# Values by pairs of heads in column groups, norms broadcast by transposes, later weight stores and another order of parts in a two-layer hybrid decoder trunk

## The chip, the cores and the metric

The kernel runs on 1 core of one Trainium2 chip. Its time is the device time of one execution in microseconds (us); lower is better. The engines are TensorE (PE in the profile; PEld is its weight load), VectorE (DVE), ScalarE (ACT), GpSimd (POOL) and SyncE (SP), which issues the DMAs.

## The reference

Two layers, each with a half-step feed-forward, a mixer of four head groups beside each other, and a second half-step feed-forward. x is 512 tokens by 1024, everything in float32.

```python
def hybrid_layer(x, ...):
    x = x + 0.5 * swiglu(rmsnorm(x, ffn1_norm), ffn1_gate, ffn1_up, ffn1_down)   # 1024 -> 2816 -> 1024
    z = rmsnorm(x, mix_norm) @ w_in
    ...
    y_a = dsa_mixer(...)    # per query the best 128 keys by an indexer, 4 heads of 64, T5 bias
    y_b = gla_mixer(...)    # gated linear attention in chunks
    y_c = conv_mixer(...)   # gated causal depthwise convolution, 31 taps
    y_d = mla_mixer(...)    # latent attention, 4 heads, values 64 wide
    x = x + concat([y_a, y_b, y_c, y_d]) @ w_out
    x = x + 0.5 * swiglu(rmsnorm(x, ffn2_norm), ffn2_gate, ffn2_up, ffn2_down)
    return x

# in both attentions, for each block of 128 queries:
    p = jax.nn.softmax(logits, axis=-1)
    return jnp.einsum('bhts,bshd->bthd', p.astype(v.dtype), v)
```

rmsnorm(x) is x * rsqrt(mean(x*x) + 1e-6) * g.

## The kernel before, in words

**Layout.** Activations lie transposed: X[k] holds 128 features by 512 tokens, k from 0 to 7. A large product is done as three passes in a rounded float32 form (fp32r): each operand is split into a high and a low part (hi, lo; `split`, L553), and hi*hi, hi*lo and lo*hi are added up in PSUM (`mm3`, L548). One such pass is one instruction of 128x512. The names of the profile: gu (gate and up) and dn (down) are the feed-forward's products, whl the split weights, xh and xl the split activations, iq, cq, ckv, cg, ca, bq, bk and g the projections of the mixers, wo the output projection, uq and ukv the second projections of attention D's queries and keys. Small products, such as those with the values, are plain float32; one of them shows as two instructions in the profile.

**Stages.** `ffn` (L688) runs 22 blocks of 128 hidden features in four parts; `mixers` (L727) projects, runs the four groups and projects back; the norm of the next stage is summed as X is written. `Norm.finish` (L620) makes the factor per token, r4, and `bcast` (L585) spreads it over the partitions as a row (bc, in the profile rbc): VectorE multiplies the identity by each column (rbcd), and PE multiplies a matrix of ones by that, 512 columns in plain float32 (rbcp). `c_out` (L1185) does the same for the convolution's norm (rcbp).

**Weights of the mixers.** They are loaded early, split once, and stored in device memory in split form (`keep`, L522: kraw, khl, kept), so that `fetch` (L538) can load them split when the mixers need them. In layer 0 the first feed-forward does three of these per hidden block (`ahead=3`, L1268), from its first block on; kraw shares its four buffers with the weights of the feed-forward (raw).

**Attention.** `d_attention(i)` (L967) and `a_attention(i)` (L1207) handle the 128 queries of block i, with 128*(i+1) keys. Per head: logits on PE (dlg; alg and blg, two heads side by side in row groups of the array), row maximum on VectorE (mx), exponential and row sum on ScalarE (dpr, apr; sm), then `attend` (L799): transposes on PE (dpT, apT), a copy to SBUF (pts), the product with the values with pts held in the array and 64 value columns streamed (dpo, apo), and a copy scaled by the reciprocal of the row sum (rs) into y (dy, ay). After four heads `y_out` (L757) transposes y (yT) and splits it into Y for wo. `best(i)` (L843) finds the 128 best keys in 16 rounds of two VectorE instructions (MAX, MATCH_REPLACE) over 128*(i+1) columns; attention A's block i needs it. Logits dlg and alg share two PSUM banks (tag s1), dpT and dpo share two others (s2), projections have four (mm).

**What sets the order.** Nothing is issued as it is written. The program records all its instructions (`Plan.record`, L179); `Plan.schedule` (L289) lays them on the engines by a table of costs and of delays between engines (`EDGE`, L102), with its own idea of the clock (`STAY`, `WAKE`, L107) and of buffers, in rounds; `Plan.run` (L420) issues the order of the round that the plan reckons shortest. The list `ORDER` (L50) gives the parts of the mixers in the order in which they are recorded, and by that the order in which they take turns at shared buffers. On each engine, instructions then run in that order.

Of the kernel before, what the change touches and what calls it, by code (L numbers as in the profile page):

```python
# [19 lines left out]
OP = mybir.AluOpType  # L20
# [20 lines left out]
RAW = 4  # L41
ROUNDS = 5
TMP = {"lg": 4, "t1": 2, "t2": 3, "ct": 1, "dd": 2, "qe": 2, "pts": 2, "yt": 3, "hp": 2, "z3": 4,  "cg": 1, "rbc": 2}
BANKS = {"mm": 4, "s1": 2, "s2": 2}
# [4 lines left out]

ORDER = ("index0 conv0 gates d_tables index1 index_keys best2 d_latent_kv best3 b_decays d_latent best1 "  # L50
         "d_queries d_keys d_room b_heads d_attention0 d_attention2 conv1 d_attention3 d_attention1 "
         "b_states a_heads b_zero b_scores3 values b_scores4 b_scores0 b_halves b_chain b_scores1 "
         "b_scores2 c_out a_bias b_out2 b_out1 a_attention3 b_out3 b_out0 b_gates a_attention0 "
         "a_attention1 b_norm a_attention2").split()

# [36 lines left out]
class _Op:  # L92
    __slots__ = ("args", "forms", "key", "cost", "lat", "tiles", "after", "succ", "n", "work", "port")


class Plan:
# [4 lines left out]

    EDGE = {"VV": 127, "VS": 128, "VP": 256, "VG": 155, "SV": 142, "SS": 220, "SP": 271, "SG": 170,  # L102
            "PV": 196, "PS": 197, "PP": 0, "PG": 200, "GV": 74, "GS": 110, "GP": 203, "GG": 102,
            "DD": 0, "VD": 150, "SD": 150, "PD": 150, "GD": 150, "DV": 170, "DS": 170, "DP": 170, "DG": 170}
    HOLD, MARGIN, KEEP = 300.0, 2000.0, "V"
    TAX = {"V": 400.0, "G": 0.0, "S": 0.0}
    WINDOW, STAY, WAKE = 4096 / 1.2, 0.37, 0.77  # L107

# [70 lines left out]
    def record(self, forms, others=(), whole=None):  # L179

        op = _Op()
        op.n = len(self.ops)
        op.forms = {f[0]: whole or (self.cost(f[0], f[1], *f[3:]),) + f[2:] for f in forms}
        op.port = {f[0] for f in forms if self.shares(f[0], f[1], f[3], f[4])}
        key, method, _, args, kw = forms[0]
        op.key, op.cost = key, op.forms[key][0]
        op.lat, op.work = 0.0, 1.0
        if method == "matmul":
# [100 lines left out]
    def schedule(self, rank):  # L289
# [14 lines left out]
        port, other = {"V": 0.0, "G": 0.0}, {"V": "G", "G": "V"}  # L304
        wire = 0.0
        left = [len(op.after) for op in ops]
# [5 lines left out]
        def choose(e):  # L312
            now, found, first = free[e], [], 1e18
            for op in ready[e]:
# [3 lines left out]
                if e in op.port and t < port[e]:  # L318
                    t = port[e]
                if t > first + self.HOLD:  # L320
                    continue
# [38 lines left out]
        while len(order) < len(ops):  # L360
# [13 lines left out]
            start[op.n] = at  # L374
            cost = op.forms[e][0]
            if e == "P":
                while at >= mark:
# [42 lines left out]
    def run(self):  # L420
# [7 lines left out]
        best = None  # L428
        for _ in range(ROUNDS):
            rank[:self.head] = [n - 1e9 for n in range(self.head)]  # L430
            time, order, start, stop, taken = self.schedule(rank)
            if best is None or time < best[0]:
# [11 lines left out]
def hybrid_trunk(ctx, tc, x_in, cst, masks, onehot, relb, pcol, prow, gu17, w_uq, w_ukv,  # L444
# [140 lines left out]
    def bcast(col, name):  # L585

        dg = tmp("pts", name + "d")
        for i in range(NT):
            V.tensor_scalar(dg[:, i * 128:(i + 1) * 128], ident, col[:, i:i + 1], None, op0=OP.mult)
        ps = bank(name + "p")  # L590
        PE.matmul(ps, ones, dg, start=True, stop=True)
        r = tmp("rbc", name)
        copy(r, ps)
        return r
# [54 lines left out]
    def build_consts():  # L649
        SP.dma_start(ck, cst)  # L650
        for l in range(1, depth):
            SP.dma_start(PC[l], pcol[l])
        V.tensor_copy(identb, ident)
        V.tensor_copy(causb, CM[:, 384:512])

    def build_masks():
        mk = tmp("hp", "mk", 640)
# [29 lines left out]

    def ffn(norm, gu, dn, after, between=lambda: None, lead=(), ahead=0):  # L688

# [9 lines left out]
        for part, n in enumerate(PARTS):  # L699
            H = []  # L700
            for m in range(m0, m0 + n):
# [10 lines left out]
                H.append((hh, hl))  # L712
                keep(ahead)
            for d in range(KD):
# [12 lines left out]
    def mixers(l, norm, after):  # L727
# [70 lines left out]

        def attend(i, h, probs, sm, values, y, name):  # L799
            W = 128 * (i + 1)  # L800
            pt = bank(name + "pT")
            for j in range(i + 1):
                PE.transpose(pt[:, j * 128:(j + 1) * 128], probs[:, j * 128:(j + 1) * 128], ident)
            rs = small("rs", 1, 4)
            V.reciprocal(rs, sm)
            pts = tmp("pts", "pts")
            copy(pts[:, :W], pt[:, :W])
            po = bank(name + "po")
            for j in range(i + 1):
                PE.matmul(po[:, :64], pts[:, j * 128:(j + 1) * 128], values(j, h), start=(j == 0), stop=(j == i))  # L810
            copy(y[:, h * 64:(h + 1) * 64], po[:, :64], rs)

# [154 lines left out]
        def d_attention(i):  # L967

            W = 128 * (i + 1)
            y = tmp("yt", "dy", 256)  # L970
            for h in range(4):
# [6 lines left out]
                S.activation(e[:, :W], p[:, :W], AF.Exp, bias=mx, accum_out=sm)  # L978
                attend(i, h, e, sm, lambda j, h: st.KV[j][:, h, 64:128], y, "d")
            y_out(y, 6, i)  # L980

# [225 lines left out]
        def a_attention(i):  # L1207

            W = 128 * (i + 1)
            y = tmp("yt", "ay", 256)  # L1210
            for h in range(4):
# [13 lines left out]
                S.activation(e[:, :W], e[:, :W], AF.Exp, bias=mx, scale=-1.0, accum_out=sm)  # L1225
                attend(i, h, e, sm, lambda j, h: st.VAB[j][:, h * 64:(h + 1) * 64], y, "a")
            y_out(y, 0, i)

# [162 lines left out]
```

## Time and profile before

| what | value |
|---|---|
| time, median of 3 runs | 2016.08 us (2015.13 to 2018.04) |
| the profiled execution: time, span | 2027.9 us, 2026.1 us |
| mean granted TensorE clock | 0.986 |
| busy: PE, DVE, ACT | 1993.3, 1271.3, 804.0 us |
| moved by DMA | 309.47 MB, mean 153 GB/s |
| ACT_TABLE_LOAD | 10 instructions, 1283 ns each |

How to read it: the span runs from the first to the last instruction of the profiled execution. Busy shares are means over stages with different limits: the four feed-forward stages and the two mixers (about 380 to 660 us and 1383 to 1660 us) have to be looked at apart. The granted clock is the share of full speed that TensorE ran at; at 0.5 a product takes twice as long and PE counts as busy all the while. A wait is put down to what came last.

### The profile page before, as it was taken

To read this page: it belongs to the slowest core of one execution; us is meant where nothing else is said; L and a number is where in the kernel's file an instruction comes from. 1 tells how busy PE (TensorE), PEld (TensorE's weight loads), DVE (VectorE), ACT (ScalarE), POOL (GpSimd) and SP (SyncE) were. 2 spreads that over 40 slices of the span, in tenths; PEclk is the share of its full clock that TensorE was granted. 3 is DMA by queue.
4 is the path that set the end of the run, shared out by engine and by line. 5 is a ranking of instruction groups with operands and counts; after the bars stand their busy time and mean duration, and the time that the engine had idled before them with its cause. 6 is when DMAs were issued, how large, how long until landed. Compare 5 with 4: busy or idle time off the path is not lost.

```text
span 2026.1 us, 26063 instructions
## 1 busy us (share of the span) xinstructions
PE 1993.3 (98%) x9428; PEld 1634.4 (81%) x9430; DVE 1271.3 (63%) x2709; ACT 804.0 (40%) x1566; POOL 7.4 (0%) x20
## 2 busy tenths in 40 slices
PE   8999999999999999999999999999999999999999
PEld 6888888877887888888888888888768778888887
DVE  7665555689895645454675546557889855454544
ACT  5343333365454423333443434333645443222322
POOL 0000000000000000000000000000000000000000
PEclk9999999989899999999999999999989999999999
DMA  8776766552332435353464737446424322323232
GB/s 309 256 259 215 233 202 213 172 165 94 109 131 94 151 118 181 117 172 116 144 218 154 227 112 257 130 146 179 153 81 125 115 94 86 108 89 113 81 107 83
DMA packets 110852, 309.47 MB, mean 153 GB/s; under 512 B 13122, under 2 KB 24676, under 8 KB 110724
## 3 DMA queue, kind: packets, MB, share of 16 engines
q1 hardware_dynamic: 110724, 307.81, 47.3%
q8 instruction: 74, 1.21, 0.2%
q14 instruction: 54, 0.44, 0.1%
HBM read 238.95 MB, written 65.67 MB: 150 GB/s over the span
## 4 chain that ended last, share of the span: by engine, by line
PE 91%; DVE 4%; ACT 2%; DMA 2%; issue 1%; SPq 0%; DVEq 0%; ACTq 0%
PE gu L440 44%; PE dn L440 24%; PE g L440 5%; PE wo L440 5%; PE cq L440 1%; PE iq L440 1%; PE cg L440 1%; PE dlg L440 1%; PE apo L440 1%; PE dpo L440 1%; PE alg L122 1%; PE ca L440 1%; DVE sc L440 1%; PE uq L440 1%; DVE c L440 1%; DMA kraw<-wo 1%
## 5 line engine op out<-in xcount | busy, mean ns | idle before, releaser
L440 PE MATMUL gu<-xh,whl 128*128 128x512 f32 x2816 | 828.6, 391 | 8.0 <-ACT whl L440 6.5
L440 PEld LDWEIGHTS gu<-xh,whl 128*128 128x128 f32 x2816 | 528.8, 188 | 120.7 <-ACT whl L440 6.5
L440 ACT ACTIVATE whl<-raw 128x512 fp32r<-128x512 f32 (+1 forms) x519 | 307.1, 594 | 670.0 <-PE gu L440 363.8
L440 PE MATMUL gu<-xl,whl 128*128 128x512 f32 x1408 | 499.0, 391 | 0.0
L440 DVE TENSOR_TENSOR whl<-raw,whl 128x512 fp32r<-128x512 f32 x576 | 369.4, 646 | 157.2 <-ACT whl L440 151.8
L440 PE MATMUL dn<-hh,whl 128*128 128x512 f32 x1408 | 426.8, 389 | 0.0
L440 PEld LDWEIGHTS gu<-xl,whl 128*128 128x128 f32 x1408 | 264.6, 188 | 55.6 <-issue 0.5
L440 PEld LDWEIGHTS dn<-hh,whl 128*128 128x128 f32 x1408 | 264.1, 188 | 55.7 <-ACT hh L440 0.5
L440 PE MATMUL dn<-hl,whl 128*128 128x512 f32 x704 | 258.4, 389 | 0.0
L440 DVE SCALAR_TENSOR_TENSOR x<-dn,x 128x512 f32<-128x512 f32 x128 | 87.8, 690 | 144.6 <-PE dn L440 144.5
L440 PEld LDWEIGHTS dn<-hl,whl 128*128 128x128 f32 x704 | 132.1, 188 | 28.0 <-issue 0.8
L440 DVE TENSOR_TENSOR fg<-gu,rbc 128x512 f32<-128x512 f32 x88 | 60.6, 689 | 120.1 <-PE gu L440 116.3
L440 DVE TENSOR_TENSOR fu<-gu,rbc 128x512 f32<-128x512 f32 x88 | 60.6, 689 | 97.4 <-PE gu L440 97.3
L440 DVE TENSOR_TENSOR khl<-kraw,khl 128x512 fp32r<-128x512 f32 (+1 forms) x124 | 81.7, 666 | 58.8 <-ACT khl L440 58.3
L440 ACT ACTIVATE khl<-kraw 128x512 fp32r<-128x512 f32 (+1 forms) x123 | 74.9, 613 | 104.0 <-DMA kept<-khl 30.9
L440 PE MATMUL g<-whl,xh 128*128 128x512 f32 (+1 forms) x384 | 101.1, 378 | 0.0
L440 ACT ACTIVATE hh<-fu 128x512 fp32r<-128x512 f32 x86 | 54.5, 634 | 95.3 <-DVE fu L440 95.0
L440 PE MATMUL wo<-yh,whl 128*128 128x512 f32 x256 | 83.1, 415 | 1.4 <-ACT yh L440 1.4
L440 DVE TENSOR_TENSOR hl<-fu,hh 128x512 fp32r<-128x512 f32 x88 | 60.7, 690 | 26.1 <-ACT hh L440 25.4
L440 PEld LDWEIGHTS g<-whl,xh 128*128 128x128 f32 x384 | 68.1, 191 | 9.2 <-ACT bd L440 0.2
L440 ACT ACTIVATE fg<-fg 128x512 f32<-128x512 f32 x88 | 55.3, 629 | 33.3 <-DVE fg L440 30.7
L440 DVE TENSOR_TENSOR fu<-fu,fg 128x512 f32<-128x512 f32 x88 | 60.5, 687 | 2.1 <-ACT fg L440 0.7
(325 smaller groups left out, 1989.6 us busy)
## 6 DMA issues: line engine op xcount, KB each, us to landing
raw<-gu SPq DMA_DIRECT2D x176, 512.0 KB, 4.3
kept<-khl SPq DMA_DIRECT2D x108, 512.0 KB, 4.3
whl<-kept SPq DMA_DIRECT2D x108, 512.0 KB, 3.7
raw<-dn SPq DMA_DIRECT2D x96, 384.0 KB, 3.2
kraw<-wt SPq DMA_DIRECT2D x44, 256.0 KB, 3.7
kraw<-wg SPq DMA_DIRECT2D x32, 256.0 KB, 5.2
kraw<-wo SPq DMA_DIRECT2D x32, 256.0 KB, 4.2
raw<-dn SPq DMA_DIRECT2D x32, 256.0 KB, 2.8
```

Source lines behind the costliest of these rows:

```text
L122: f[2](*f[3], **f[4])
L440: call(*args, **kw)
```

## The change

**Values.** `attend` is split in two. `weigh` takes the reciprocal, scales the probabilities by it, transposes them and copies them to pts. After every second head the new `attend` holds the two heads' values (128 keys by 64) in the two column halves of the array and streams each head's pts (128 queries), so that the outputs of two heads come out transposed, one in partitions 0 to 63 and one in 64 to 127, and are split straight into Y. The copies dy and ay, the buffer yt and the transposes yT of both attentions go (the one of group B stays). pts gets a third buffer.

**Broadcast.** `bcast` makes the row by four PE transposes of a column read 128 times over; the product with ones and its four multiplications go.

**Start.** The constants are loaded in two pieces, the 128 columns of the identity first, and `keep` begins with the third hidden block (`since=2`).

**Plan.** Other delays between engines, another pair of clock thresholds, and a price for a change of table on ScalarE: an activation whose table is not the loaded one is put off by 1280 in the plan's reckoning. Four rounds instead of five, and the fourth one's order is taken (`PICK = 3`) whatever the plan reckons of it. `ORDER` is another permutation: best3 comes ahead of best2 and best1, the kv part of attention D after its query part, a_heads after b_scores3, and attention A's blocks in the order 2, 0, 1, 3 instead of 3, 0, 1, 2.

```diff
-ROUNDS = 5
-TMP = {... "pts": 2, "yt": 3, ...}
+ROUNDS, PICK = 4, 3
+TMP = {... "pts": 3, ...}
...
-    EDGE = {"VV": 127, "VS": 128, "VP": 256, "VG": 155, "SV": 142, "SS": 220, "SP": 271, "SG": 170,
+    EDGE = {"VV": 127, "VS": 128, "VP": 160, "VG": 155, "SV": 142, "SS": 220, "SP": 170, "SG": 170,
...
-    WINDOW, STAY, WAKE = 4096 / 1.2, 0.37, 0.77
+    WINDOW, STAY, WAKE = 4096 / 1.2, 0.40, 0.76
+    TABLES, SWITCH = {AF.Exp: 1, AF.Tanh: 1, AF.Silu: 2, AF.Ln: 3}, 1280.0
...
+                if e == "S" and op.table and op.table != table and t < now + self.SWITCH:
+                    t = now + self.SWITCH
...
     def bcast(col, name):
-        dg = tmp("pts", name + "d")
+        ps = bank(name + "p")
         for i in range(NT):
-            V.tensor_scalar(dg[:, i * 128:(i + 1) * 128], ident, col[:, i:i + 1], None, op0=OP.mult)
-        ps = bank(name + "p")
-        PE.matmul(ps, ones, dg, start=True, stop=True)
+            PE.transpose(ps[:, i * 128:(i + 1) * 128], col[:, i:i + 1].to_broadcast([128, 128]), ident)
...
     def build_consts():
-        SP.dma_start(ck, cst)
+        SP.dma_start(ident, cst[:, C_ID:C_ID + 128])
+
+    def build_masks():
+        SP.dma_start(ck[:, 128:], cst[:, 128:])
...
-                keep(ahead)
+                if m >= since:
+                    keep(ahead)
...
-        def attend(i, h, probs, sm, values, y, name):
+        def weigh(i, probs, sm, name):
             W = 128 * (i + 1)
+            rs = small("rs", 1, 4)
+            V.reciprocal(rs, sm)
+            copy(probs[:, :W], probs[:, :W], rs)
             pt = bank(name + "pT")
             for j in range(i + 1):
                 PE.transpose(pt[:, j * 128:(j + 1) * 128], probs[:, j * 128:(j + 1) * 128], ident)
-            rs = small("rs", 1, 4)
-            V.reciprocal(rs, sm)
             pts = tmp("pts", "pts")
             copy(pts[:, :W], pt[:, :W])
+            return pts
+
+        def attend(i, pts, values, y, name):
             po = bank(name + "po")
-            for j in range(i + 1):
-                PE.matmul(po[:, :64], pts[:, j * 128:(j + 1) * 128], values(j, h), start=(j == 0), stop=(j == i))
-            copy(y[:, h * 64:(h + 1) * 64], po[:, :64], rs)
+            plan.together(200 + 2 * 150 * (i + 1),
+                          *[PE.form("matmul", po[64 * n:64 * n + 64, :128], values(j, n), pts[n][:, j * 128:(j + 1) * 128],
+                                    start=(j == 0), stop=(j == i)) for j in range(i + 1) for n in range(2)])
+            t = slice(i * 128, (i + 1) * 128)
+            split(po[:, :128], y[0][:, t], y[1][:, t])
...
-            y_out(y, 6, i)
+                pts.append(weigh(i, e, sm, "d"))
+                if h % 2:
+                    attend(i, pts[h - 1:], lambda j, n: st.KV[j][:, h - 1 + n, 64:128], Y[6 + h // 2], "d")
...
-            ffn(norm, gu1[l], dn1[l], nm.add, build_masks, lead, ahead=3)
+            ffn(norm, gu1[l], dn1[l], nm.add, build_masks, lead, ahead=3, since=2)
```

How the order moves is shown at three places of layer 0.

The first is on ScalarE, at the gates of group B (la: a logarithm of a sigmoid, by way of Exp and Ln; bcum: its running sum; kd: exponentials of it) and the split of the weights for attention D's queries (shi is the high part that PE's uq holds). Before:

```order
L440 ACTIVATE la_886<-la_886 128x512
L440 ACT_TABLE_LOAD
L440 ACTIVATE la_886<-la_886 128x512
L440 ACTIVATE lsq<-cq 128x512 x2
L440 ACTIVATE rl<-isc 128x256 x2
L440 ACTIVATE bcum<-bcum 128x512
L440 ACTIVATE rl<-isc 128x256
L440 ACTIVATE cqh<-cq,pc_71 128x512
L440 ACT_TABLE_LOAD
L440 ACTIVATE kd<-bcum 128x128 x3
L440 ACTIVATE shi<-raw 128x384
```

The same place now:

```order
L446 ACTIVATE la_890<-la_890 128x512
L446 ACT_TABLE_LOAD
L446 ACTIVATE la_890<-la_890 128x512
L446 ACTIVATE lsq<-ckv 128x512
L446 ACTIVATE bcum<-bcum 128x512
L446 ACTIVATE ckvh<-ckv,pc_71 128x512
L446 ACTIVATE shi<-raw 128x384 x2
L446 ACTIVATE dq<-uq,cqu 128x384 x4
```

The third table load and the three kd moved behind both shi; they now come after the copies dkv of attention D's keys. The indexer's rl of the 256-wide block moved away too.

The second place is on PE, at attention D's block of 512 keys (dlg the logits, the product of causb and identb adds the mask, dpT the transposes, dpo the values). Before:

```order
L440 MATMUL dlg<-dkT_1001,dqT_966 128x512
L440 LDWEIGHTS identb
L440 MATMUL dlg<-causb,identb 128x128
L440 MATMUL dpT<-ck,dpr 128x128 x4
L440 MATMUL dlg<-dkT_1002,dqT_967 128x512
L440 LDWEIGHTS identb
L440 MATMUL dlg<-causb,identb 128x128
L440 MATMUL dpo<-dkv,pts 128x64 x3
L440 MATMUL dpT<-ck,dpr 128x128 x4
L440 MATMUL dpo<-dkv,pts 128x64
L440 MATMUL dlg<-dkT_1003,dqT_968 128x512
```

Now, at the end of the same block's logits and the start of the next block's:

```order
L446 MATMUL dlg<-dkT_1009,dqT_932 128x512
L446 MATMUL dpT<-ck,dpr 128x128 x4
L446 LDWEIGHTS identb
L446 MATMUL dlg<-causb,identb 128x128
L446 MATMUL g_1185<-whl,xl_707 128x512
L446 MATMUL g_1187<-whl,xh_700 128x512
L446 MATMUL g_1188<-whl,xh_700 128x512
L446 MATMUL g_1186<-whl,xh_706 128x512
L446 MATMUL dlg<-dkT_1006,dqT_929 128x384
L446 MATMUL dpT<-ck,dpr 128x128 x4
```

The projection products g (attention A's queries and keys) moved in among attention D's: 31 of them stand ahead of the first dlg and 88 between the first dlg and the last dpo. Before, the first g came after three of the four blocks.

The third place is on VectorE, where attention A begins (ISA apr,mx is the fused bias and row maximum of one head). Before, it stood among the parts of group B:

```order
L440 SCALAR_TENSOR_TENSOR yl_1312<-cth,yh_1311 128x512
L440 ISA apr,mx<-alg,z_1317 128x512
L440 ISA mx 128x1
L440 ISA apr,mx<-blg,z_1318 128x512
L440 ISA mx 128x1
L440 TENSOR_REDUCE bss<-bsq 128x4
L440 RECIPROCAL rs<-sm 128x1
```

Now:

```order
L446 MATCH_REPLACE sc_953<-c_976,sc_953 128x256
L446 ISA apr,mx<-alg,z_1304 128x384
L446 ISA mx 128x1
L446 ISA apr,mx<-blg,z_1305 128x384
L446 ISA mx 128x1
L446 COPY bon<-bo 128x256
L446 RECIPROCAL rs<-sm 128x1
L446 MAX c_977<-sc_953 128x8
L446 RECIPROCAL rs<-sm 128x1
L446 MATCH_REPLACE sc_953<-c_977,sc_953 128x256
```

The 256-wide rounds of best1, which before ran beside attention D, moved to the start of attention A, whose first block is now the one of 384 keys.

More of the change, by code (lines that the diff above doesn't have):

```diff
@@ L41 @@
 RAW = 4
-ROUNDS = 5
-TMP = {"lg": 4, "t1": 2, "t2": 3, "ct": 1, "dd": 2, "qe": 2, "pts": 2, "yt": 3, "hp": 2, "z3": 4,  "cg": 1, "rbc": 2}
+ROUNDS, PICK = 4, 3
+TMP = {"lg": 4, "t1": 2, "t2": 3, "ct": 1, "dd": 2, "qe": 2, "pts": 3, "hp": 2, "z3": 4,  "cg": 1, "rbc": 2}
 BANKS = {"mm": 4, "s1": 2, "s2": 2}
@@ L48 @@
 GROUPS, EARLY = ((6, 7), (4, 5), (2, 3), (0, 1)), (0, 1)
[L50 to L54, printed above, removed]
+ORDER = ("index0 conv0 gates index1 index_keys best3 best2 d_latent d_tables b_decays d_latent_kv "
+         "d_queries b_heads best1 d_keys d_room d_attention1 conv1 d_attention3 d_attention2 d_attention0 "
+         "b_zero b_scores3 a_heads b_states values b_scores4 b_halves b_scores0 b_chain b_scores1 c_out "
+         "b_scores2 b_gates b_out2 b_out0 b_out3 a_bias a_attention2 a_attention0 b_out1 a_attention1 "
+         "b_norm a_attention3").split()
 AQ, AK, AV = 0, 256, 512
@@ L92 @@
 class _Op:
-    __slots__ = ("args", "forms", "key", "cost", "lat", "tiles", "after", "succ", "n", "work", "port")
+    __slots__ = ("args", "forms", "key", "cost", "lat", "tiles", "after", "succ", "n", "work", "port", "table")
 class Plan:
-    EDGE = {"VV": 127, "VS": 128, "VP": 256, "VG": 155, "SV": 142, "SS": 220, "SP": 271, "SG": 170,
+    EDGE = {"VV": 127, "VS": 128, "VP": 160, "VG": 155, "SV": 142, "SS": 220, "SP": 170, "SG": 170,
             "PV": 196, "PS": 197, "PP": 0, "PG": 200, "GV": 74, "GS": 110, "GP": 203, "GG": 102,
@@ L187, in record @@
         op.lat, op.work = 0.0, 1.0
+        op.table = self.TABLES.get(args[2]) if method == "activation" else None
         if method == "matmul":
@@ L304, in schedule @@
         port, other = {"V": 0.0, "G": 0.0}, {"V": "G", "G": "V"}
-        wire = 0.0
+        wire, table = 0.0, None
         left = [len(op.after) for op in ops]
@@ L375, in schedule @@
             cost = op.forms[e][0]
+            if e == "S" and op.table:
+                table = op.table
             if e == "P":
@@ L428, in run @@
         best = None
-        for _ in range(ROUNDS):
+        for turn in range(ROUNDS):
             rank[:self.head] = [n - 1e9 for n in range(self.head)]
             time, order, start, stop, taken = self.schedule(rank)
-            if best is None or time < best[0]:
+            if turn == PICK if PICK is not None else best is None or time < best[0]:
                 best = (time, order, taken)
@@ L654, in build_consts @@
         V.tensor_copy(causb, CM[:, 384:512])
-    def build_masks():
         mk = tmp("hp", "mk", 640)
@@ L685, in rel_bias_tiles, with ffn @@
         return Z
-    def ffn(norm, gu, dn, after, between=lambda: None, lead=(), ahead=0):
+    def ffn(norm, gu, dn, after, between=lambda: None, lead=(), ahead=0, since=0):
         lead, m0 = list(lead), 0
@@ L969, in d_attention @@
             W = 128 * (i + 1)
-            y = tmp("yt", "dy", 256)
+            pts = []
             for h in range(4):
@@ L978, in d_attention @@
                 S.activation(e[:, :W], p[:, :W], AF.Exp, bias=mx, accum_out=sm)
-                attend(i, h, e, sm, lambda j, h: st.KV[j][:, h, 64:128], y, "d")
-            y_out(y, 6, i)
+                pts.append(weigh(i, e, sm, "d"))
+                if h % 2:
+                    attend(i, pts[h - 1:], lambda j, n: st.KV[j][:, h - 1 + n, 64:128], Y[6 + h // 2], "d")
         def b_heads():
@@ L1209, in a_attention @@
             W = 128 * (i + 1)
-            y = tmp("yt", "ay", 256)
+            pts = []
             for h in range(4):
@@ L1225, in a_attention @@
                 S.activation(e[:, :W], e[:, :W], AF.Exp, bias=mx, scale=-1.0, accum_out=sm)
-                attend(i, h, e, sm, lambda j, h: st.VAB[j][:, h * 64:(h + 1) * 64], y, "a")
-            y_out(y, 0, i)
+                pts.append(weigh(i, e, sm, "a"))
+                if h % 2:
+                    attend(i, pts[h - 1:], lambda j, n: st.VAB[j][:, (h - 1 + n) * 64:(h + n) * 64], Y[h // 2], "a")
         parts = dict(gates=gates, index_keys=index_keys, d_latent=d_latent, d_latent_kv=d_latent_kv, d_tables=d_tables, d_queries=d_queries,
```

## The prediction

> **What bounds the kernel now.** I read the page first: the share of each engine and the chain that ended last.
>
> ```profile
> span 2026.1 us, 26063 instructions
> ...
> PE 1993.3 (98%) x9428; PEld 1634.4 (81%) x9430; DVE 1271.3 (63%) x2709; ACT 804.0 (40%) x1566; POOL 7.4 (0%) x20
> ...
> PE 91%; DVE 4%; ACT 2%; DMA 2%; issue 1%; SPq 0%; DVEq 0%; ACTq 0%
> ```
>
> TensorE (PE) is the bound: 98% busy, 91% of the chain. A busy PE is not yet a fast one, so I then read the busy time and the granted clock stage by stage (each row: stretch, its length, busy us of each engine, then the clock PEclk, the DMA share, GB/s).
>
> ```profile
> 100.00:150.00 50.00, 50.00 (x222) 41.40 (x221) 30.97 (x50) 20.31 (x35) 0.00 (x0) 1.00 0.76 253
> 440.00:460.00 20.00, 16.01 (x72) 14.43 (x71) 14.19 (x56) 14.94 (x31) 0.00 (x0) 0.74 0.27 92
> 480.00:520.00 40.00, 36.08 (x177) 26.83 (x175) 33.35 (x105) 19.22 (x63) 0.00 (x0) 0.79 0.14 40
> 510.00:520.00 10.00, 9.47 (x39) 8.41 (x39) 6.57 (x18) 2.70 (x7) 0.00 (x0) 0.50 0.01 2
> 590.00:640.00 50.00, 49.67 (x300) 38.02 (x300) 28.68 (x108) 25.74 (x82) 0.00 (x0) 1.00 0.35 111
> 1440.00:1460.00 20.00, 15.36 (x79) 13.62 (x79) 15.21 (x54) 14.79 (x29) 0.00 (x0) 0.83 0.38 126
> 1480.00:1520.00 40.00, 35.88 (x173) 26.14 (x172) 33.72 (x104) 19.03 (x62) 0.00 (x0) 0.79 0.14 46
> ```
>
> The first row is a feed-forward stage: full clock, never idle, 222 products in 50 us, that is 0.225 us each. Nothing can be won there but by fewer products. The mixers of each layer have two holes. In each I count as lost the idle time plus busy time x (1 - clock).
> - Hole A (440 to 460 and, in layer 1, 1440 to 1460): 3.99 + 16.01 x 0.26 = 8.2 us, and 4.64 + 15.36 x 0.17 = 7.3 us.
> - Hole B (480 to 520 and 1480 to 1520): 3.92 + 36.08 x 0.21 = 11.5 us, and 4.12 + 35.88 x 0.21 = 11.7 us. From 510 to 520 PE is 95% busy and still at half clock.
>
> Together 38.7 us. What PE waited for there, from the list of waits (total us, times, longest):
>
> ```profile
> PE gu L440 <- ACT whl L440: 6.5, 1, 6.5
> PE uq L440 <- ACT shi L440: 4.5, 2, 2.6
> PE isc L440 <- DVE bla L440: 4.0, 2, 2.0
> PE dlg L440 <- DVE yl L440: 2.8, 2, 1.4
> ```
>
> The first is the start of the program. The next two are hole A, once per layer; the last is hole B.
>
> **Hole A, the order on ScalarE.** ScalarE's timeline of the hole (start us, us):
>
> ```profile
> 439.36 1.28 ACT L440 ACT_TABLE_LOAD   x1
> ...
> 441.30 1.28 ACT L440 ACT_TABLE_LOAD   x1
> ...
> 447.33 1.28 ACT L440 ACT_TABLE_LOAD   x1
> 448.63 0.99 ACT L440 ACTIVATE kd<-bcum 128x128 f32<-128x128 f32 x3
> 449.52 0.51 ACT L440 ACTIVATE shi<-raw 128x384 fp32r<-128x384 f32 x1
> ```
>
> The query products uq need shi, and shi stood behind a table load and three exponentials: 1.28 + 0.99 = 2.3 us. After the change shi comes ahead of both, and PE has 21 ckv products between la and bcum where it had 11 cq (10 more, 2.2 us). These two answer the waits on shi and on bla. What is late next is slo, the low half of the same weights: VectorE makes the second one behind rounds of the top-k search. I let 3.5 us per layer stay (one wait of about 2 us, and the half clock beside it). Gain 15.5 - 7.0 = 8.5 us; ends 0 and 13.
>
> **Hole B, the order on PE.** Products of attention with their waits are all that PE has there (rows of PE's timeline):
>
> ```profile
> 509.54 1.91 PE L440 MATMUL dpo<-dkv,pts 128*128 128x64 f32 x8
> ...
> 518.30 1.20 PE L440 MATMUL g<-whl,xh 128*128 128x512 f32 x2
> ```
>
> The first projection product g starts at 518.30, after three of the four attention blocks. In the order after the change 88 g products lie between the first logits and the last values product of attention D, and none of that stretch's first three blocks had one before (some cg and ca at its start are all): 88 x 0.225 = 20 us of work at full rate, against 11.6 us lost per layer. They can start because conv1's and b_heads' four banks are emptied earlier: VectorE does bq, bk, cgt and cat ahead of the attention's row maxima, and 16 rounds of best1 wait until attention A, where VectorE has room (28.68 us busy of 50 from 590). I let 4 us per layer stay, since some 15 rows around the 512-wide block still hold no g. Gain 23.2 - 8.0 = 15 us; ends 0 and 21. At 640 to 650 a smaller loss stays as it is: the last values product still feeds the last products of wo.
>
> **The values in column groups.** Counts from the groups by line (x160 instructions are 80 products, two instructions each), prices from PE's timeline at full clock (a run lasts from its start to the next row's):
>
> ```profile
> L440 PE MATMUL dpo<-dkv,pts 128*128 128x64 f32 x160 | 29.7, 317 | 1.5 <-ACT pts L440 1.4
> ...
> L440 PE MATMUL apo<-vab,pts 128*128 128x64 f32 x160 | 24.3, 260 | 0.4 <-ACT pts L440 0.4
> ...
> L440 PE MATMUL yT<-ck,dy 128*128 128x128 f32 x16 | 4.7, 304 | 1.1 <-ACT dy L440 1.1
> ...
> L440 PE MATMUL yT<-ck,ay 128*128 128x128 f32 x16 | 4.5, 283 | 0.6 <-ACT ay L440 0.6
> ```
>
> ```profile
> 584.69 1.12 PE L122 MATMUL ba<-bf 32*128 32x64 f32 x32
> 585.74 0.50 PE L440 MATMUL wo<-yh,whl 128*128 128x512 f32 x1
> ...
> 586.77 1.02 PE L440 MATMUL rcbp<-rcbd,ones 128*128 128x512 f32 x2
> 587.63 0.59 PE L440 MATMUL bo<-bst,qd 128*128 128x256 f32 x2
> ...
> 590.20 0.95 PE L440 MATMUL wo<-yh,whl 128*128 128x512 f32 x3
> 591.07 0.69 PE L122 MATMUL alg<-aT,aT 64*128 64x512 f32 x1
> ...
> 594.91 0.60 PE L440 MATMUL apT<-ck,apr 128*128 128x128 f32 x4
> 595.26 0.71 PE L440 MATMUL wo<-yh,whl 128*128 128x512 f32 x2
> ...
> 605.89 1.00 PE L440 MATMUL apo<-vab,pts 128*128 128x64 f32 x8
> 606.72 0.28 PE L440 MATMUL yT<-ck,ay 128*128 128x128 f32 x1
> 607.74 0.37 PE L122 MATMUL alg<-aT,aT 64*128 64x128 f32 x1
> ...
> 607.95 0.27 PE L122 MATMUL alg<-aT,aT 64*128 64x128 f32 x1
> ```
>
> Now: 8 instructions from 605.89 to 606.72, 0.104 us each. The same 320 instructions remain, with 64 columns held and 128 streamed, two heads in the two halves of the array. No row shows that form. Two row groups (alg and blg at 128 columns) take 0.21 us a pair, 0.105 each; four row groups (ba) 32 in 1.05 us, 0.033 each. Bounds: 320 x (0.104 - 0.033) = 23 us won, or nothing on the products. Against it stands the entry into a grouped run: wo's three products end their turn at 590.20 + 3 x 0.225 = 590.88 and alg starts at 591.07, 0.2 us. 32 runs at up to 0.2 us cost at most 6 us. I take 0.085 us an instruction, near the two-group row, and 0.1 us a run: 320 x 0.019 - 3.2 = 3 us won; ends -6 and +23.
>
> The Trainium skill, TensorEngine Tiling, under Tiling Modes, says that a change of tiling mode drains TensorE, which speaks against this edit; the 0.2 us ahead of alg agrees. By that rule at both ends of each run the term would be 6.1 - 12.8 = -7 us, and the whole sum 24 us instead of 34.
>
> The 32 transposes yT of attention's outputs go: four transposes take 0.35 us (apT, 594.91 to 595.26), 0.09 each, 3 us in all; ends 2 and 9 (their mean durations, 0.3 us). The 64 scalings move from 64-wide outputs to probabilities up to 512 wide, and stand ahead of the transposes: each waits for VectorE's reciprocal, and behind it on ScalarE wait the next exponentials and pts copies, behind the transposes on PE the next logits and g. ScalarE is 40% busy, and the g products cover the longer chain: nothing. If that cover is gone, it is the first rival.
>
> **Norms by transposes.** Eight broadcasts: the product against ones takes 0.86 us (586.77 to 587.63), four transposes 0.35 us. All eight lie where PE is the bound: 8 x 0.5 = 4 us; ends 0 and 5. The eight times four multiplications on VectorE go too, off the path.
>
> **Start and weight stores.** The third and fourth weight blocks are issued ahead of the stores and of most constants; the relp products that filled that wait move to the end of the stage, where PE is full. SP's queue carries the same bytes, and PE never waited for a DMA after the start: 0, ends -1 and +2.
>
> **Sum** for the two layers: 8.5 + 15 + 3 + 3 + 4 = 33.5 us. The profiled execution took 2027.9 us (span 2026.1 and 1.8 around it), 11.8 us over the median of 2016.08; 0.6% of 33.5 us is nothing, so I take it off the median unscaled: 2016.1 - 33.5 = 1982.6, say 1983.
>
> **The rivals.**
> 1. *The wait moves.* Reciprocal and scaling lengthen each head's chain; the values wait for two heads, and logits have two banks. Then hole B stays whole and half of A's gain goes: 4 + 3 + 3 + 4 = 14 us, 2002. For it: PE waited for ScalarE and VectorE there already. Against it: 88 products of filler. 0.22.
> 2. *More is won.* Both holes close (38.7) and the column groups run nearer to ba's price (+10): 38.7 + 10 + 3 + 4 = 56 us, 1960. 0.10.
> 3. *Same.* The holes move elsewhere in the mixers and the new grouping costs what the rest wins. 2016. 0.05.
> 4. *Slower: attention A falls to half clock.* From 590 to 640 PE ran at 1.00 because dense wo products lay between the attention's. The g products spent early, and best1's rounds now queued on VectorE between A's row maxima, can leave A's blocks waiting as B's did from 501 to 518. Work at half clock takes twice its time: with k us of it per layer the change costs 2k against 33.5, so it decides from k = 17 of those 50 us; with half of them (25) it gives 2016 - 33.5 + 50 = 2033. Against it: the order still has wo between all of A's blocks. 0.08. The Trainium skill, TensorE: Matmul & The Clock Gate, Part 1, has a clock that falls after an idle window of some 3.4 us. This trace differs: half clock at 95% busy (510 to 520). By that rule A, hardly idle, could not fall, and this rival would have no chance.
>
> **How the numbers follow.** The forecast, 1983, has 0.55, with 1972 to 1995 of its own from the ends above. Leaving out the fourth rival, the third and the lower part of the second, the range is 1966 to 2010. A measurement of this kernel can tell about 0.2%, 4 us, from no change. Faster: 0.55 + 0.22 + 0.10 = 0.87; within 0.2%: 0.05; slower: 0.08.
>
> **What would show it.** In the profile after: clock near 1.00 and g rows in PE's timeline between the logits of attention D; no wait of uq for shi over 1 us; runs of 16 grouped instructions in 1.5 us or less; rbcp in four short rows. The forecast is wrong if the mixers' stretches still hold more than 25 us of lost time over both layers, if the grouped rows take over 0.12 us each, or if the clock falls after 580.

## The result and the profile after

The change made the kernel faster: 1985.47 us, median of 4 runs (1984.81 to 1989.97), against 2017.06 us (2015.13 to 2026.59); ratio 0.984, 95% interval 0.980 to 0.987. The forecast was 1983. The total is right; two groups of its terms are not, and they cancel, as the runs below show: the holes gave less than forecast, the products more.

From the page of the profile after (span; busy time of each engine; share of the chain that ended last):

```profile
span 1983.0 us, 25919 instructions
...
PE 1962.0 (99%) x9412; PEld 1596.5 (81%) x9414; DVE 1262.6 (64%) x2676; ACT 815.9 (41%) x1567; POOL 7.3 (0%) x20
...
PE 96%; DVE 2%; ACT 1%; DMA 1%; issue 0%; SPq 0%; ACTq 0%; DVEq 0%
```

Stretch by stretch (length, busy us of each engine, PEclk, DMA share, GB/s). Hole A is now spread over 420 to 460 and 1400 to 1440 (in the second layer it also comes earlier, since all before it is shorter). In the kernel before, PE was never idle from 420 to 440 and from 1400 to 1440, at full clock:

```profile
360.00:380.00 20.00, 20.00 (x64) 12.19 (x63) 12.78 (x21) 8.62 (x17) 0.12 (x1) 0.83 0.61 200
420.00:460.00 40.00, 36.55 (x168) 28.27 (x169) 36.82 (x96) 25.28 (x48) 0.64 (x2) 0.96 0.47 145
480.00:520.00 40.00, 40.00 (x232) 29.59 (x230) 39.85 (x136) 23.11 (x67) 0.00 (x0) 1.00 0.33 106
590.00:640.00 50.00, 49.47 (x282) 37.30 (x282) 36.31 (x114) 29.54 (x75) 0.00 (x0) 1.00 0.33 112
1400.00:1440.00 40.00, 35.37 (x154) 27.58 (x153) 34.79 (x91) 22.41 (x40) 0.00 (x0) 0.91 0.45 135
1480.00:1520.00 40.00, 40.00 (x246) 28.40 (x245) 38.22 (x112) 32.32 (x83) 1.98 (x4) 1.00 0.36 115
```

Hole B is gone: PE is never idle there, at full clock. Hole A is not: 3.45 + 36.55 x 0.04 = 4.9 us and 4.63 + 35.37 x 0.09 = 7.8 us are still lost. And there is a loss that the forecast did not have, from 360 to 380: PE is busy all the time and yet at 0.83, 3.4 us.

The 43.1 us between the two spans split into three parts. Idle time of PE went from 32.8 us (span less busy) to 21.0: 11.8. The half clock (busy time x what is missing to 1.00, summed over rows of 20 us; two rows at 0.99, 0.4 us together, are left out) went from 23.5 to 8.0: 15.5. What is left, products at full clock, went from 1993.3 - 23.5 to 1962.0 - 8.0: 15.8.

The profiled execution of the kernel before was one of its longest. In nine to thirteen runs beside each experiment it took 2015 to 2028 us (medians of 2019 to 2022), and time and granted clock went together: 2016.42 us at 0.993, 2026.50 us at 0.988, and 0.005 x 2020 us is just the 10.1 us between them. So most of what differs from run to run is half clock. No trace of a shorter execution of this kernel was kept, so where in it the half clock is missing is not shown.

What PE waits for now (total us, times, longest):

```profile
PE isc L446 <- ACT rl L446: 1.7, 3, 0.7
PE isc L446 <- DVE bla L446: 1.6, 1, 1.6
PE cq L446 <- DMA whl<-kept: 1.0, 2, 0.8
PE bcum L446 <- DVE bla L446: 0.8, 1, 0.8
PE uq L446 <- DVE slo L446: 0.7, 2, 0.4
PE uq L446 <- ACT shi L446: 0.7, 2, 0.5
```

The wait of uq for shi fell from 4.5 to 0.7 us, and that of isc for bla from 4.0 to 1.6. What is left are many short waits. One of them is on the chain of the decays on ScalarE (start us, us): from la at 442.56 to the end of the third one stand two table loads of 1.28 us, as before, and the sum bcum waits for what VectorE makes of it. New are waits for weights that a DMA brings: 1.0 us of cq and 0.6 of g.

```profile
442.56 0.60 ACT L446 ACTIVATE la<-la 128x512 f32<-128x512 f32 x1 [1.36 <-PE la L446]
443.18 1.28 ACT L446 ACT_TABLE_LOAD   x1
444.47 0.63 ACT L446 ACTIVATE la<-la 128x512 f32<-128x512 f32 x1
445.12 1.28 ACT L446 ACT_TABLE_LOAD   x1
446.42 0.63 ACT L446 ACTIVATE la<-la 128x512 f32<-128x512 f32 x1
```

The grouped values, from PE's timeline of attention D (start us, us; a run lasts to the next row's start):

```profile
503.69 0.66 PE L123 MATMUL dpo<-pts,dkv 128*64 128x128 f32 x8
504.27 1.12 PE L446 MATMUL dlg<-dkT,dqT 96*128 96x512 f32 x2
...
508.74 0.47 PE L446 MATMUL g<-whl,xl 128*128 128x512 f32 x1
...
512.20 1.09 PE L123 MATMUL dpo<-pts,dkv 128*64 128x128 f32 x16
513.23 0.23 PE L446 MATMUL dlg<-causb,identb 128*128 128x128 bf16 x1
```

Eight instructions take 0.58 us and sixteen 1.03: 0.056 us each and 0.13 us once per run (runs of four and twelve, 0.37 and 0.81 us, fit that). The old form took 0.104 each in its runs of eight. Between them stand the g products that the order put there.

### The profile page after: what moved, and what is told of

It is laid out like the page before. It is cut to its first block, busy times and chain, and to the rows that moved or that the text cites. A ratio compares the mean times of both kernels' runs of the same rounds, so it can differ in the third digit from the quotient of the medians.

```text
span 1983.0 us, 25919 instructions
## 1 busy us (share of the span) xinstructions
PE 1962.0 (99%) x9412; PEld 1596.5 (81%) x9414; DVE 1262.6 (64%) x2676; ACT 815.9 (41%) x1567; POOL 7.3 (0%) x20
## 4 chain that ended last, share of the span: by engine, by line
PE 96%; DVE 2%; ACT 1%; DMA 1%; issue 0%; SPq 0%; ACTq 0%; DVEq 0%
PE gu L446 48%; PE dn L446 24%; PE g L446 6%; PE wo L446 4%; PE iq L446 1%; PE dlg L446 1%; PE cg L446 1%; PE ca L446 1%; PE alg L123 1%; DMA whl<-kept 1%; PE apo L123 1%; PE dpo L123 1%; PE bk L446 1%; PE bq L446 1%; PE ba L123 1%; PE cq L446 1%
## 5 line engine op out<-in xcount | busy, mean ns | idle before, releaser
L446 ACT ACTIVATE whl<-raw 128x512 fp32r<-128x512 f32 (+1 forms) x542 | 319.5, 593 | 686.4 <-PE gu L446 406.7
L446 PE MATMUL g<-whl,xh 128*128 128x512 f32 (+1 forms) x384 | 107.2, 380 | 0.6 <-DMA whl<-kept 0.6
```

What stands on the lines that cost most here:

```text
L446: call(*args, **kw)
```

## The experiments

**The order or the rewritten attentions?** The first two runs cross the two halves of the change. The planner lays all instructions anew in each, so that neither has exactly the order of the other kernel. e1_old_order is the kernel after with ORDER and the planner's settings of before (its main lines; EDGE goes back too):

```diff
-ROUNDS, PICK = 4, 3
+ROUNDS, PICK = 5, None
...
-ORDER = ("index0 conv0 gates index1 index_keys best3 best2 ...
+ORDER = ("index0 conv0 gates d_tables index1 index_keys best2 ...
...
-    WINDOW, STAY, WAKE = 4096 / 1.2, 0.40, 0.76
+    WINDOW, STAY, WAKE = 4096 / 1.2, 0.37, 0.77
-    TABLES, SWITCH = {AF.Exp: 1, AF.Tanh: 1, AF.Silu: 2, AF.Ln: 3}, 1280.0
+    TABLES, SWITCH = {}, 1280.0
```

> The kernel after with the kernel before's order of parts and planner settings; the values in column groups, the transposed norms, the start and the weight stores stay as changed. Theory 1 (the holes are closed by the order): some 22 of the 31.6 us are lost again, about 2007 us (2001 to 2014); PE falls back to half clock in attention D, and g products are again missing between its blocks. Theory 2 (the rewrite of the attentions itself brought the time): 1985 to 1993 us, and the clock in attention D stays at 1.00 without g products.

Measured: 2000.27 us (1997.27 to 2001.46), ratio to before 0.989 (0.987 to 0.991); before, beside it, 2021.51 (11 runs). That is between the two theories. Its stretches:

```profile
420.00:460.00 40.00, 35.34 (x165) 30.03 (x164) 33.62 (x98) 28.39 (x54) 0.57 (x2) 0.87 0.38 126
480.00:520.00 40.00, 38.12 (x219) 25.81 (x218) 40.00 (x129) 25.60 (x76) 0.00 (x0) 1.00 0.24 80
1480.00:1520.00 40.00, 38.84 (x217) 27.07 (x216) 38.68 (x118) 22.34 (x55) 0.00 (x0) 0.96 0.21 67
```

Hole A is as large as in the kernel before (4.66 + 35.34 x 0.13 = 9.3 us in layer 0; uq waits 5.3 us for shi again), but hole B is nearly closed: 1.9 and 2.7 us lost. PE's timeline there shows not one g product between 494.87 and 506.41, and full clock all the same:

```profile
494.87 2.02 PE L446 MATMUL dlg<-dkT,dqT 96*128 96x512 f32 x4
...
497.87 1.30 PE L123 MATMUL dpo<-pts,dkv 128*64 128x128 f32 x12
499.51 1.12 PE L446 MATMUL dlg<-dkT,dqT 96*128 96x512 f32 x2 [0.35 <-ACT dpr L446]
...
502.74 1.58 PE L123 MATMUL dpo<-pts,dkv 128*64 128x128 f32 x16 [0.19 <-ACT pts L446]
...
506.41 0.50 PE L446 MATMUL g<-whl,xh 128*128 128x512 f32 x1
```

e2_order_alone is the other half: the kernel before with the new ORDER, settings and pinned round (the + lines of the diff above, the other way round).

> The kernel before with only the new order of parts and the new planner settings; values by single heads with their own transposes, norms broadcast by products against ones, old start. Theory 1 (the order closes the holes): about 1995 us (1990 to 2002), clock 1.00 in attention D. Theory 2 (the rewrite of the attentions brought the time): 2009 to 2017 us, half clock still in attention D.

Measured: 2032.89 us (2028.26 to 2035.94), ratio 1.006 (1.0045 to 1.0081): slower than the kernel before. Neither theory had that. Its trace:

```profile
PE isc L446 <- DVE bla L446: 6.5, 2, 4.3
...
PE apo L446 <- ACT pts L446: 2.6, 4, 0.7
PE apT L446 <- ACT apr L446: 2.5, 5, 1.2
```

```profile
480.00:520.00 40.00, 37.74 (x198) 28.38 (x197) 39.80 (x137) 17.32 (x52) 0.00 (x0) 1.00 0.34 103
1480.00:1520.00 40.00, 38.08 (x186) 28.58 (x184) 39.51 (x132) 19.26 (x54) 0.00 (x0) 0.91 0.29 92
```

With g products between the old blocks hole B shrinks too (2.3 us in layer 0 at full clock, 5.3 in layer 1). But isc now waits 6.5 us for bla (4.0 in the kernel before), and attention A's old chain waits, where it hardly did. So in these traces each half of the change closes most of hole B by itself (23.2 us before, 4.6 with e1, 7.6 with e2, none with both); the two gains there do not add. How much of the 23.2 a shorter execution of the kernel before has is not shown: 15 of it are half clock, and this is what varies. The idle time alone went from 8.0 us to 3.0 with e1 and 4.2 with e2. By the medians ORDER and the settings are worth some 15 us under the new attentions (2000.27 to 1985.47; 10 by the ratios to before) and cost some 11 under the old (2021.51 to 2032.89).

**What the column halves bring.** e3_head_after_head issues the same instructions, head after head (the end of the line in `attend`):

```diff
-  ... for j in range(i + 1) for n in range(2)])
+  ... for n in range(2) for j in range(i + 1)])
```

> The kernel after with the values of a pair issued head after head instead of in turn, so that neighbouring products fall into the same half of the columns; nothing else is changed, the order of all other instructions neither. Theory 1 (the two halves run beside each other, 0.064 us an instruction in runs of 16): without that the 320 instructions cost 0.10 us or more, 320 x 0.04 = 12 us: about 1997 us (1993 to 2003). Theory 2 (128 columns streamed against 64 held are cheap by themselves): within 3 us of 1985.5.

Measured: 1988.93 us (1987.25 to 1989.60), 3.5 more than the kernel after at the median; by the ratios to before (0.9837 and 0.9839) the two are not told apart. That is near theory 2's number, but the timeline bears out theory 1. Runs of 4 and 8 take what they took in turn (0.37 and 0.59 us); runs of 12 take 1.08 us for 0.81 and runs of 16 take 1.52 for 1.03, 6.1 us more over the eight of each:

```profile
502.17 0.66 PE L123 MATMUL dpo<-pts,dkv 128*64 128x128 f32 x8
502.77 1.12 PE L446 MATMUL dlg<-dkT,dqT 96*128 96x512 f32 x2
...
510.68 1.58 PE L123 MATMUL dpo<-pts,dkv 128*64 128x128 f32 x16
512.20 0.23 PE L446 MATMUL dlg<-causb,identb 128*128 128x128 bf16 x1
```

The starts of the single instructions in the trace say why. In turn they start two at a time, a pair every 0.11 us. In e3's runs of 16 the first and the last ones start singly, 0.11 us apart, and those between start two in 0.11 us again; its runs of 4 and 8 start in pairs throughout. So the edit took away only part of what it was to take away: to all appearance (a record does not name its half) PE begins the second head's instructions while the first head's are still running. Where one half works alone, an instruction costs 0.11 us, as in the old form. The form by itself is not cheap; the gain comes from the two halves working at the same time.

e6_values_twice issues each run twice, all other instructions in the same order:

```diff
-  ... for j in range(i + 1) for n in range(2)])
+  ... for _ in range(2) for j in range(i + 1) for n in range(2)])
```

> The kernel after with every grouped run of values products issued twice (the second pass writes the same sums again), 320 instructions more; the order of all others is the same. Theory 1 (a grouped instruction costs 0.055 to 0.07 us, and all of it lies where PE is the bound): 18 to 22 us more, 2003 to 2008 us. Theory 2 (the prediction's price of 0.085 us holds, with the waits around a run added to it): 2011 to 2016 us. Theory 3 (a good part of the runs lies beside waits for the next head): under 2000 us.

Measured: 2000.22 us (1998.34 to 2003.41), 14.7 more; PE's busy time grew by 17.5 us, that is 0.055 us an instruction. Between the two profiled executions the span grew by 16.7 us and idle time fell by 0.8, so nearly all of it lies where PE is the bound:

```profile
PE 1979.5 (99%) x9734; PEld 1615.9 (81%) x9734; DVE 1265.6 (63%) x2676; ACT 815.8 (41%) x1567; POOL 7.1 (0%) x20
```

The time lies just below theory 1's range, and the price far below the prediction's 0.085.

**The norms.** e4_ones_norms takes back the broadcast alone:

```diff
-            PE.transpose(ps[:, i * 128:(i + 1) * 128], col[:, i:i + 1].to_broadcast([128, 128]), ident)
...
+            V.tensor_scalar(dg[:, i * 128:(i + 1) * 128], ident, col[:, i:i + 1], None, op0=OP.mult)
...
+        PE.matmul(ps, ones, dg, start=True, stop=True)
```

> The kernel after with the eight norms broadcast by a product against ones again, with their four multiplications on VectorE each. Theory 1 (they lie where PE is the bound, 8 x 0.5 us): about 1989.5 us (1987 to 1993). Theory 2 (half of their products lie beside other waits, or the longer chain through VectorE opens a wait): 1985 us, or over 1993 us with a new wait for VectorE in front of what follows the norms.

Measured: 1999.80 us (1999.21 to 2000.25), 14.3 more than the kernel after. Only 4.5 of it are products (1969.7 us busy less 11.2 of half clock, against 1954.0). The rest is 6.6 us of idle time and 3.2 of half clock, and its longest wait, in the second layer's hole A, lies nowhere near a norm (1.6 us in the kernel after):

```profile
PE 1969.7 (99%) x9398; PEld 1600.7 (80%) x9398; DVE 1270.9 (64%) x2713; ACT 812.8 (41%) x1562; POOL 9.0 (0%) x20
```

```profile
PE isc L446 <- DVE bla L446: 6.6, 2, 5.5
```

The planner lays all instructions anew when a few change, and the fourth round's order is taken whatever it is. So about 10 us of this difference seem to be the order's, not the broadcast's; the run gives the broadcast 4.5 us of products but does not time it alone.

**The start.** e5_start_undone loads the constants in one piece again and stores kept weights from the first block on:

```diff
-        SP.dma_start(ident, cst[:, C_ID:C_ID + 128])
...
+        SP.dma_start(ck, cst)
...
-            ffn(norm, gu1[l], dn1[l], nm.add, build_masks, lead, ahead=3, since=2)
+            ffn(norm, gu1[l], dn1[l], nm.add, build_masks, lead, ahead=3)
```

> The kernel after with the start undone: all constants in one transfer right behind the second weight block, and the kept weight halves stored from the first step of the first feed-forward stage on; order, planner settings, values and norms as in the kernel after. Theory 1 (the start is worth nothing, as forecast): within 4 us of 1985.5. Theory 2 (the third and fourth weight blocks come some us earlier in the kernel after, and PE waits less over the first 25 us): 1988 to 1995 us, with over 2 us more of idle PE in that stretch. Theory 3 (the products for the bias table, moved by the change into a full stretch, cost more than the earlier blocks bring): 1980 to 1983 us.

Measured: 1989.97 us (1987.60 to 1995.34), ratio 0.987 (0.985 to 0.989) against 0.984 (0.980 to 0.987) for the kernel after: the intervals overlap. PE is idle 8.4 us in the first 20, against 7.2, and not at all from 20 to 40: less than theory 2 asked for. But from 20 to 40 the clock is at 0.83 with PE busy all the time, 3.4 us, where the kernel after has 1.00; from 24 to 29, just ahead of the fall, PE runs ten of the instructions for the bias table. Here too the plan laid the rest anew. Whether the start is worth nothing or a few us stays open.

**Why the clock falls.** The loss from 360 to 380 has no idle time in it. There PE runs the bias table's products relp on 32 of the 128 rows of the array: 14 of their 16 instructions stand from 364 to 377, where before 8 stood at that place:

```profile
371.01 2.07 PE L446 MATMUL relp<-oh,rbb 32*128 32x512 f32 x2
373.01 1.22 PE L446 MATMUL dn<-hh,whl 128*128 128x512 f32 x2
```

e7_quarter_rows and e8_all_rows issue each of them eight times, the one on 32 rows (BUCKETS), the other on 128, where the added rows hold zeros (`form[1]` in place of `form[0]`); the two have the same order of instructions on every engine:

```diff
-                PE.matmul(ps[:, :b - a], rbb[:BUCKETS, h * 128:(h + 1) * 128], oh[:BUCKETS, a:b], start=True, stop=True)
+                form = [PE.form("matmul", ps[:, :b - a], rbb[:n, h * 128:(h + 1) * 128], oh[:n, a:b], start=True, stop=True)
+                        for n in (BUCKETS, 128)]
...
+                def call(f=form[0]):
+                    for _ in range(8):
+                        f[2](*f[3], **f[4])
...
```

> The kernel after with each of the 16 products for the bias table issued eight times in a row, with 32 rows of the array at work as now. All else equal to the next kernel, which does the same with 128 rows (the added rows hold zeros). Both add 56 products 512 wide and 56 products 128 wide, 30 to 42 us at full clock, and no idle time. Theory 1 (the clock falls when little of the array works, even with PE never idle): half clock in several of these stretches, 10 to 40 us longer than the kernel with 128 rows. Theory 2 (the clock falls only after idle time): no half clock there, within 4 us of the kernel with 128 rows.

> The same eightfold products for the bias table with all 128 rows of the array at work (zeros in the added rows), instructions in the same order. Theory 1 and theory 2 alike: full clock in these stretches, 2015 to 2028 us. If these stretches fall to half clock too, neither theory holds.

Measured: 2043.00 us (2042.20 to 2047.22) on 32 rows, 2018.42 (2016.54 to 2024.03) on 128; mean clock 0.982 and 0.993 in the profiled executions. On 32 rows, sixteen instructions (one product, eight times) take 10.3 us, and the clock goes to one half:

```profile
359.89 10.36 PE L685 MATMUL relp<-oh,rbb 32*128 32x512 f32 x16
370.19 1.22 PE L446 MATMUL gu<-xh,whl 128*128 128x512 f32 x2
```

```profile
360.00:364.00 4.00, 4.00 (x9) 1.66 (x10) 0.69 (x1) 0.45 (x1) 0.00 (x0) 0.95 0.46 131
364.00:368.00 4.00, 4.00 (x6) 1.64 (x5) 0.00 (x0) 0.00 (x0) 0.00 (x0) 0.50 0.00 0
```

In another stretch of the same kernel it is 0.66 over 20 us, PE never idle:

```profile
380.00:400.00 20.00, 20.00 (x45) 10.99 (x44) 2.95 (x5) 3.10 (x5) 0.00 (x0) 0.66 0.15 50
```

On 128 rows the same sixteen take 6.5 us, at full clock:

```profile
368.00:378.00 10.00, 10.00 (x31) 5.60 (x30) 1.11 (x3) 1.25 (x3) 0.00 (x0) 1.00 0.21 66
```

```profile
369.14 7.03 PE L685 MATMUL relp<-oh,rbb 128*128 128x512 f32 x16
375.61 1.04 PE L446 MATMUL dn<-hh,whl 128*128 128x512 f32 x2
```

Theory 1 holds: 24.6 us between two kernels that differ only in the rows at work. Over the rows of 20 us that hold these products (20 to 60 and 360 to 440) half clock costs 22.7 us on 32 rows and nothing on 128; elsewhere it costs about the same in both (11.4 and 11.8 us). The plan of both kernels of this change reckons in this way already: it counts a product's work as its rows over 128 (`op.work`) when it works out its idea of the clock.

**What is left of hole A.** e9_two_loads_less takes the two table loads out of the chain, everything else in the same order (the lines with `table` make the plan reckon with them all the same):

```diff
-            S.activation(t1, t1, AF.Exp, scale=-1.0)
-            S.activation(t1, t1, AF.Ln, bias=1.0)
+            S.activation(t1, t1, AF.Abs)
+            plan.ops[-1].table = 1
+            S.activation(t1, t1, AF.Abs)
+            plan.ops[-1].table = 3
```

> The kernel after, with the exponential and the logarithm of the decays replaced by two absolute values of the same size, so that the two table loads of 1.28 us between la and bla go (this leaves the decays out of the computation); the order on all engines is the same otherwise. Theory 1 (what is left of hole A hangs on the chain from la over two table loads to bcum): the waits of isc and bcum for bla (1.6 and 0.8 us) go, and the half clock beside them: of the 12.7 us lost from 420 to 460 and from 1400 to 1440 about half comes back, 1979 us (1976 to 1982). Theory 2 (rl, shi and slo are late right behind it): 1983 to 1987 us, and the waits stand at those names.

Measured: 1983.01 us (1982.13 to 1984.13), 2.5 less than the kernel after at the median; the intervals of the two ratios to before overlap (0.978 to 0.983 here). The waits for bla are gone and isc still waits 1.7 us for rl and uq for shi, now 1.4: theory 2. From 420 to 460 and from 1400 to 1440 still 11.8 of the 12.7 us are lost, since half clock also comes without the waits for bla:

```profile
440.00:460.00 20.00, 19.15 (x84) 15.28 (x84) 17.00 (x52) 8.30 (x16) 0.00 (x0) 0.78 0.28 92
```

e10_load_early keeps the computation and starts the first of the two loads early:

```diff
             copy(bg[0:16, :], pgt[:16, :])
+            if 'S' in plan.ops[-1].forms:
+                behind('S', S.form('activation', small('et', 1)[:16], bg[0:16, 0:1], AF.Exp))
```

(`behind`, new too, issues it with the copy, as one step of the plan.)

> The kernel after with one exponential of a single column on ScalarE right behind the copy of bg, so that the first of the two table loads runs while ScalarE waits for the la products; nothing else moves. Theory 1 (the chain sets hole A): 1.28 us less per layer, with the clock beside it 2 to 6 us in all, 1982 us (1979 to 1984). Theory 2: within 1.5 us of 1985.5.

Measured: 1983.49 us (1982.13 to 1988.28). That is 2.0 less at the median, but the interval of its ratio to before (0.978 to 0.983) overlaps that of the kernel after; not told apart.

**Both small edits.** e11_load_early_all_rows adds the products on 128 rows. In it the clearing of the added rows also clears the table's constant, so the positions' bias is left out.

> The same with the 16 products for the bias table over all 128 rows of the array (zeros in the added rows), each issued once. Theory 1 (products on 32 rows let the clock fall in some executions, as from 370 to 376 in the profile after): 0 to 3.5 us under the kernel with the early load alone, 1980 us (1977 to 1983), and no half clock from 360 to 380. Theory 2 (that fall has another cause): the same time as the kernel with the early load alone.

Measured: 1981.97 us (1980.68 to 1984.00). e12_both_small has the constant loaded with its zeros instead (here against the kernel after, the main lines):

```diff
-        SP.dma_start(oh[:BUCKETS], onehot)
+        SP.dma_start(oh, onehot)
...
```

> The kernel after with the early table load of e10_load_early and with the bias table's products over all 128 rows, each once, the added rows zero (the constant is loaded with its zeros). Theory 1 (both small changes count as measured): 1982 us (1979 to 1984), no half clock from 360 to 380. Theory 2 (neither does): 1985.5 us, as the kernel after.

Measured: 1979.94 us (1976.48 to 1980.69), ratio to before 0.979 (0.9765 to 0.9819). That interval still touches the one of the kernel after (0.9804 to 0.9873), but its slowest run is under the fastest of that kernel (1984.81), and from 360 to 380 the clock stays up:

```profile
360.00:380.00 20.00, 20.00 (x88) 15.60 (x87) 17.60 (x28) 11.32 (x21) 0.12 (x1) 1.00 0.71 231
```

It has the lowest median of all versions here. One profile does not time the cure of 360 to 380: e3, with the products on 32 rows in the order of the kernel after, has 1.00 there too. What the rows do is shown by e7 and e8.

## Why the prediction was right, and where it wasn't

- **Bound and size.** PE is the bound, 96% of the chain now. The forecast's 33.5 us stand against 31.6 measured. That it came so near is in part luck: the holes gave some 9 us less than forecast and the products some 6 more.
- **Taking the sum off the median unscaled** failed. The profiled execution lay 11.8 us over the median, and the prediction called the scaling nothing. But its two largest terms were made of half clock in good part, and by the granted clocks of the runs that is what made this execution long. If all of it was half clock, take 11.8 us from its 23.5 of half clock and add to the 8.0 after the 0.7 by which that profiled execution lies under its median, and half clock gives 11.7 - 8.7 = 3.0 us. With 11.8 of idle time that is 14.8 us at the median, where 23.5 were forecast for the holes. The products gave 15.8, where 10 were forecast. Together 30.6.
- **Hole A**, 8.5 forecast, 15.5 to 12.7 us in the profiles: 2.8. The named wait went as said (shi 4.5 to 0.7 us). The step that failed is "what is late next is slo" with 3.5 us a layer left. Late next are bla and rl (1.6, 0.8 and 1.7 us in the waits; slo only 0.7), and the clock still falls. The 21 ckv products between la and bcum are there in layer 0, but in layer 1 only 15, and there isc waits 1.6 us for bla. Taking away the waits for bla is worth 2.5 us at the median, not clear of noise (e9).
- **Hole B**, 15 forecast, 23.2 in the profiles. The clock stays at 1.00 and g stands between the blocks, as said. That the g products are the reason is half true: e1 has none there and keeps full clock in layer 0 with the new values and norms alone (that it is their shorter chain is not shown), e2 has the g products with the old values and keeps it in layer 0. The two were forecast as separate terms; in the traces either one pays for most of this hole.
- **Values**, 3 forecast with 0.085 us an instruction and 0.1 a run. Measured 0.056 and 0.13: 22.4 us for the 32 runs, eight each of 0.37, 0.59, 0.81 and 1.03. At full clock the old form took 0.16, 0.37, 0.61 and 0.83 us for a head of 2, 4, 6 and 8 instructions, 16 of each: 31.5 us (the forecast took the 0.104 of a run of 8 for all). So 9.1 were won, three times the term. The step that failed is the price "near the two-group row": the two column halves work at the same time, a pair in the 0.11 us that one instruction takes alone (e3). TensorEngine Tiling of the Trainium skill says under Tiling Modes that a change of mode drains TensorE. That shows at most as the 0.13 us per run; the sum that the prediction made by that rule, 7 us lost on this term, is refuted.
- **Transposes and scaling.** The 32 yT are gone. The longer chain of each head costs next to nothing: the largest wait for a scaled probability in the kernel after is 0.2 us (apT for apr). Rival 1 did not come.
- **Norms**, 4 forecast; e4's products give 4.5. With the values' 9.1 and the 3 us of yT that makes 16.6 against 15.8 from the rows.
- **Start**, 0 forecast: open (e5). The prediction saw that relp moves into a full stretch (half of it; the other half stood there already), but not that 32 rows can cost the clock: 3.4 us in the profiled execution. And PE now does wait for a DMA behind the start, 1.6 us for the kept weights.
- **Rival 4** did not come: attention A ran at 1.00 (590 to 640). But its premise, that the clock can fall on a busy PE, holds for products on 32 rows. The Trainium skill, TensorE: Matmul & The Clock Gate, Part 1, lets the clock fall after an idle window; e7 has no idle time where it falls.
- **Rival 3 in another shape.** The order alone is slower than before (e2). That an order made for one set of instructions can lose on another was in none of the cases.

## What to carry to other kernels

When a stall has two cures in one change, forecast the pair and not the sum, and cross them on the chip: one run with each alone. Before a sum made on one profiled execution is taken off a median, look whether the terms are of the kind that varies from run to run; here it was mostly the half clock. Where a planner lays the order, an edit of a few instructions is timed with the whole new order: pin the order, or read the edit's own price in busy time. And when an edit is to take an overlap away, look in the trace whether it did: e3 left much of it in place, and its small cost alone would have named the wrong cause.

## What was not expected of the hardware

- The clock falls on a fully busy TensorE when few rows of the array work: 0.50 from 364 to 368 with PE busy 4.00 of 4.00 us on 32 rows, 1.00 with 128 rows, in the same order of instructions. Zeros in the added rows are enough to keep it up.
- Two column halves work at the same time, a pair of instructions (64 columns held, 128 streamed, plain float32) in 0.11 us, where one alone takes 0.11. Issued head after head they still do so in part: runs of 4 and 8 take the same 0.37 and 0.59 us, a run of 16 takes 1.52 us for 1.03.
